# New duration estimates, and new ranks and lookaheads, for the list scheduler of a two-layer hybrid encoder

## The chip, the cores and the metric

The kernel runs as one program on one core of a Trainium2 chip. The metric is the device time of one execution in microseconds (us). Five instruction streams of the core matter here: TensorE (PE in the profile, with PEld for its weight loads), VectorE (DVE), ScalarE (ACT), GpSimd (POOL) and SyncE (SP), which issues the DMAs. Each takes its instructions in the order in which the program gives them; semaphores tie the streams together.

## The reference, cut to what matters

The input x is (1, 512, 1024) float32; there are two layers. Each layer is

```
proj = h @ w_in                      # 1024 -> A 512 | B 512 | C 512 | D 352
o_a  = silu(LN(conv31(a * sigmoid(a'))))            # group A, depthwise, width 31
o_b  = softmax(rope(rms(q)) rope(rms(k))^T / 8) v   # group B, 4 heads of 64, 2 kv heads
o_c  = u * (W_s LN(v) + b), gelu before             # group C, chunks of 128 positions
o_d  = softmax(q_d k_d^T) v_d                       # group D, 4 heads, low-rank q and kv
h    = LN(alpha * h + concat(o_a..o_d) @ w_out)
up   = conv3(h @ ffn_w_up)                          # 1024 -> 2 x 2816
h    = LN(alpha * h + (silu(up_1) * up_2) @ ffn_w_down)
```

All of it is float32. The kernel holds float32 accuracy by splitting both factors of a product in a high part (rounded to fp32r) and a low part (the rest), and by three matmuls for each product: high by high, low by high, high by low.

## The kernel before

**Tiles.** The 512 positions are four tiles of 128 (`h` 0 to 3 in the program; the lists of instructions call their buffers h_83 to h_86). Weights come from HBM in chunks of two 512-column pieces, into three `raw` buffers. For each piece ACT writes the high part (`wh<-raw`), and DVE the low part (`wl<-raw,wh`); for the chunks of U, V and O (two low-rank matrices of group D, and the output projection) POOL writes the low part. Activations are transposed by PE into PSUM (`wk<-ident,h`) and split there by ACT and DVE into `hh` and `hl`. PSUM holds four `acc` and four `wk` buffers.

**Work of a layer.** Sections, in the order of the program: the projections `b`, `a`, `d`; `b_rope` (square roots `ny` on DVE, scalings `by` on ACT, products `bz` on DVE and `bw` on POOL), `b_heads`; `d_norm`, `d_lat`, `d_up` (group D's low-rank products; its rotary key products `kr` are small POOL operations); `b_att`; `c` (projection and gelu), `c_norm` (`svh`, `svl`), `c_sgu`; `d_att`; `conv` (62 DVE operations `aconv` in two chains, on the two halves of group A), `a_norm`, which begins with PE's transposes of `aconv`; then `out` (output projection and layer norm), `ffn` and `down`. In an attention, two heads go as a pair: for each, scores into `acc`, a maximum (`max<-acc`, DVE), exponentials with their sums (`prob<-acc,max`, ACT), transposes, split (`pth` on ACT, `ptl` on DVE), product with v, `bo` or `do`; at the end of a pair the sums' reciprocals `rec` and `mixh`, `mixl`. The spatial weights of `c_sgu` are split once in a layer: `sguh` on ACT, `sgul` on DVE.

**What sets the order.** Nothing is issued while the program is written: `Sched.record` notes 3830 operations with what they read and write. `Sched.place` then puts them in one order, as a list scheduler: it keeps a clock for each engine, takes for every operation the duration that `Sched.cost` gives it, and picks on each engine, among the operations that could begin first, the one with the lowest priority number. That number is the operation's place in the program plus the `rank` of its section; for weight splits it is the place at which a chunk `lead` chunks earlier is first used. `ahead` says how many chunks before its use a chunk's DMA may be issued, `window` how far from the oldest open operation an operation may be. `Sched.issue` issues the result (line 610, where all instructions of the trace stand). On the chip each engine keeps that order, and waits where its operands are not there yet; the numbers of `cost` have no other effect.

Of the kernel before, what the change touches and what calls it, by code (L numbers as in the profile page):

```python
# [48 lines left out]
for _k in KEYS:  # L49
# [22 lines left out]
TUNE = {'window': 334,  # L72
         'slack': 0.0,
         'spare': 1,
         'ahead': {'A': 6,
                   'B': 10,
                   'D': 10,
                   'U': 21,
                   'V': 12,
                   'C': 44,  # L80
                   'O': 5,
                   'F': 2,
                   'W': 6,
                   'W1': 35,
                   'W0': 15,
                   'C0': 42,
                   'A1': 17,
                   'V0': 17,
                   'C1': 42,
                   'F1': 6,  # L90
                   'A0': 30,
                   'B1': 34,
                   'D0': 9,
                   'F0': 5,
                   'B0': 27,
                   'V1': 28,
                   'U1': 32,
                   'U0': 40,
                   'D1': 5},
         'lead': {'A': 32,  # L100
                  'B': 14,
                  'D': 45,
                  'U': 73,
                  'V': 8,
                  'C': 0,
                  'O': 5,
                  'F': 37,
                  'W': 8,
                  'D1': 5,
                  'A0': 11,  # L110
                  'U1': 69,
                  'C1': 11,
                  'O1': 0,
                  'D0': 22,
                  'B1': 15,
                  'F1': 16,
                  'O0': 2,
                  'U0': 84,
                  'V1': 15,
                  'V0': 15,  # L120
                  'C0': 13,
                  'B0': 3,
                  'F0': 45,
                  'A1': 30,
                  'W0': 14,
                  'W1': 6},
         'rank': {'.0': 23,
                  '.1': -404,
                  '.3': -339,
                  'a0': 33,  # L130
                  'a1': 72,
                  'a_norm0': -14,
                  'b0': -1,
                  'b0.0': -212,
                  'b0.1': 256,
                  'b0.2': 81,
                  'b0.3': -477,
                  'b1': -618,
                  'b1.2': -365,
                  'b1.3': 59,  # L140
                  'b_att0': 142,
                  'b_att0.00': -455,
                  'b_att0.01': 19,
                  'b_att0.0n': 962,
                  'b_att0.10': -33,
                  'b_att0.1n': 49,
                  'b_att1': 24,
                  'b_att1.00': -25,
                  'b_att1.01': -10,
                  'b_att1.1n': 8,  # L150
                  'b_heads0': -527,
                  'b_heads0.0': 159,
                  'b_heads0.1': -3,
                  'b_heads1': 182,
                  'b_heads1.0': -174,
                  'b_heads1.1': -110,
                  'b_heads1.2': -4,
                  'b_rope0': -265,
                  'b_rope1': 794,
                  'c0': 78,  # L160
                  'c0.0': -15,
                  'c0.1': 6,
                  'c0.3': -638,
                  'c1': -66,
                  'c1.0': -131,
                  'c1.1': -9,
                  'c1.3': 150,
                  'c_norm0': 237,
                  'c_norm1': -16,
                  'c_sgu0': -22,  # L170
# [152 lines left out]
class Sched:  # L323
# [121 lines left out]
    def cost(eng, method, args, kw, outs, ins):  # L445
# [5 lines left out]
        n = max([v.arr.size for v in views])  # L451
# [1079 lines left out]
```

## Time and profile before

| | |
|---|---|
| time, median of 3 runs | 1155.11 us (1154.3 to 1155.8) |
| the profiled execution | 1155.01 us, of which the profile's span is 1153.2 us |
| busy: PE, DVE, ACT, POOL | 1131.9, 771.0, 558.2, 169.4 us |
| PE instructions | 5802 matmuls and transposes |

The span is what the profile sees; some 1.8 us of the execution lie around it. An engine's busy time says how much work it has, not what it is worth: the two layers alternate between stretches with different limits, so each is read by itself.

### The profile page before, as it was taken

What the parts mean: (1) busy time and instruction counts of PE and PEld (TensorE: products, weight loads), DVE (VectorE), ACT (ScalarE), POOL (GpSimd) and SP (SyncE); (2) the same over time, 40 slices, a digit from 0 to 9 for tenths busy, and PEclk for the clock granted to TensorE, in tenths of its full rate; (3) what the DMA queues carried; (4) which work ended last, traced back from release to release, by engine and by line L of the source; (5) the groups of instructions that cost most, each with busy time, mean ns of one, the idle gap of its engine ahead of it and who ended that gap; (6) DMA issues with size and microseconds to landing.
All of it is one profiled execution on the core that took longest, in us unless ns stands there. A gap on an engine that the chain in (4) does not pass through costs nothing.

```text
span 1153.2 us, 15412 instructions
## 1 busy us (share of the span) xinstructions
PE 1131.9 (98%) x5802; PEld 959.7 (83%) x5802; DVE 771.0 (67%) x1307; ACT 558.2 (48%) x1203; POOL 169.4 (15%) x203
## 2 busy tenths in 40 slices
PE   6999999999999999999999999999999999999997
PEld 5888888988888888888889877889888888888886
DVE  7799996776666755245667999777776656551425
ACT  5759794254444543224254679733564444431221
POOL 5324324100000001000112734320000000000002
PEclk9999999999999999999999999999999999999999
DMA  6520022233233532135232002122353223231311
GB/s 228 165 74 20 19 92 74 74 97 104 92 92 109 167 106 79 55 110 166 95 124 68 7 20 58 53 92 73 128 164 111 92 92 110 74 110 42 105 56 73
DMA packets 32041, 105.71 MB, mean 92 GB/s; under 512 B 3680, under 2 KB 4064, under 8 KB 31968
## 3 DMA queue, kind: packets, MB, share of 16 engines
q1 hardware_dynamic: 31968, 104.74, 27.7%
q8 instruction: 45, 0.74, 0.3%
q14 instruction: 28, 0.23, 0.1%
HBM read 102.63 MB, written 2.10 MB: 91 GB/s over the span
## 4 chain that ended last, share of the span: by engine, by line
PE 90%; ACT 5%; DVE 2%; DMA 1%; issue 1%; POOL 0%; SPq 0%; DVEq 0%; ACTq 0%
PE acc L610 55%; PE wk L610 35%; ACT prob L610 2%; ACT pth L610 1%; ACT wh L610 1%; DVE ptl L610 1%; ACT c L610 1%; DVE aconv L610 0%; DMA raw<-in_wst_dram 0%; DMA h<-in_x_dram 0%; ACT do L610 0%; DVE max L610 0%; DVE bo L610 0%; ACT mixh L610 0%; ACT bo L610 0%
## 5 line engine op out<-in xcount | busy, mean ns | idle before, releaser
L610 DVE TENSOR_TENSOR wl<-raw,wh 128x512 fp32r<-128x512 f32 (+1 forms) x264 | 171.6, 688 | 85.6 <-ACT wh L610 60.6
L610 ACT ACTIVATE wh<-raw 128x512 fp32r<-128x512 f32 (+2 forms) x310 | 176.1, 615 | 67.8 <-DMA raw<-in_wst_dram 60.8
L610 PE MATMUL acc<-hh,wh 128*128 128x512 f32 (+1 forms) x544 | 191.8, 353 | 0.0
L610 PE MATMUL acc<-hh,wl 128*128 128x512 f32 (+1 forms) x544 | 191.2, 352 | 0.0
L610 PE MATMUL acc<-hl,wh 128*128 128x512 f32 (+1 forms) x544 | 191.2, 352 | 0.0
L610 PE MATMUL wk<-hh,wh 128*128 128x512 f32 x320 | 124.5, 389 | 0.0
L610 PE MATMUL wk<-hl,wh 128*128 128x512 f32 x320 | 124.5, 389 | 0.0
L610 PE MATMUL wk<-hh,wl 128*128 128x512 f32 x320 | 124.5, 389 | 0.0
L610 PEld LDWEIGHTS acc<-hh,wl 128*128 128x128 f32 x544 | 102.8, 189 | 13.8
L610 PEld LDWEIGHTS acc<-hl,wh 128*128 128x128 f32 x544 | 102.9, 189 | 13.6
L610 PEld LDWEIGHTS acc<-hh,wh 128*128 128x128 f32 x544 | 102.9, 189 | 13.6
L610 POOL TENSOR_TENSOR vr<-ve,mhalf 128x1 f32<-128x1 f32 (+2 forms) x26 | 25.4, 977 | 534.6 <-DVE ve L610 534.5
L610 DVE SCALAR_TENSOR_TENSOR y<-acc,pp,y 128x511 f32<-128x511 f32 x96 | 71.6, 749 | 37.2 <-ACT y L610 35.4
L610 DVE TENSOR_TENSOR hl<-raw,hh 128x512 fp32r<-128x512 f32 x56 | 37.7, 689 | 84.3 <-ACT hh L610 84.2
L610 ACT ACTIVATE hh<-raw 128x512 fp32r<-128x512 f32 x56 | 34.9, 630 | 111.5 <-PE acc L610 93.5
L610 DVE SCALAR_TENSOR_TENSOR aconv<-aglu,pp,aconv 128x501 f32<-128x501 f32 (+14 forms) x120 | 86.7, 758 | 0.6
L610 PE MATMUL acc<-hl,fh 128*128 128x512 f32 x224 | 85.8, 383 | 0.0
L610 PE MATMUL acc<-hh,fh 128*128 128x512 f32 x224 | 85.7, 383 | 0.0
L610 PE MATMUL acc<-hh,fl 128*128 128x512 f32 x224 | 85.7, 382 | 0.0
L610 DVE SCALAR_TENSOR_TENSOR y<-wk,pp,y 128x511 f32<-128x511 f32 x80 | 60.0, 750 | 33.7 <-ACT y L610 31.9
L610 PE MATMUL wk<-wh,hh 128*128 128x512 f32 (+1 forms) x192 | 73.7, 384 | 0.0
L610 POOL TENSOR_TENSOR wl<-raw,wh 128x512 fp32r<-128x512 f32 (+1 forms) x46 | 59.8, 1320 | 91.6 <-ACT wh L610 58.3
(201 smaller groups left out, 2290.5 us busy)
## 6 DMA issues: line engine op xcount, KB each, us to landing
raw<-in_wst_dram SPq DMA_DIRECT2D x172, 512.0 KB, 3.5
row<-in_rows_dram SPq DMA_DIRECT2D x16, 256.0 KB, 5.0
raw<-in_wst_dram SPq DMA_DIRECT2D x8, 352.0 KB, 3.0
out_dram<-h SPq DMA_DIRECT2D x8, 256.0 KB, 2.0
h<-in_x_dram SPq DMA_DIRECT2D x3, 512.0 KB, 5.2
raw<-in_wst_dram SPq DMA_DIRECT2D x2, 384.0 KB, 3.8
h<-in_x_dram SPq DMA_DIRECT2D x2, 256.0 KB, 3.1
raw<-in_wst_dram SPq DMA_DIRECT2D x2, 256.0 KB, 3.1
```

The source lines that it names most:

```text
L610: f(*[a.real() if isinstance(a, View) else a for a in args], **{k: v.real() if isinstance(v, View) else v for k, v in kw.items()})
```

## The change

It edits two things: the estimates in `cost`, and the tables in `TUNE` that `place` uses. An exponential over 512 columns with its sum now counts 30 ns above its plain cost in place of 115. A POOL product counted 150 ns plus 1.66 or 2.1 ns for an element; it now counts 150 ns up to 8 elements, and 320 ns plus 1.4 or 1.8 ns for an element above. `window`, 20 of the 25 `ahead` numbers, all `lead` numbers and nearly all `rank` entries are new.

```diff
-TUNE = {'window': 334,
+TUNE = {'window': 591,
...
-                   'C0': 42,
+                   'C0': 62,
...
-            return ((50.0 if from_psum else 94.0) + n / 1.2 + 72.0 * ptrs + (115.0 if "accum_out" in kw else 0.0),
+            return ((50.0 if from_psum else 94.0) + n / 1.2 + 72.0 * ptrs + ((30.0 if n == 512 else 115.0) if "accum_out" in kw else 0.0),
                     118.0 if from_psum else 95.0, False)
         if ALU.pow in args:
             return 700.0 + n * 145.0, 40.0, True
         narrow = any(0 in v.arr.strides for v in ins)
-        return 150.0 + n * (1.66 if narrow and n == 512 else 2.1), 40.0, True
+        if n <= 8:
+            return 150.0, 40.0, True
+        return 320.0 + n * (1.4 if narrow and n == 512 else 1.8), 40.0, True
```

The same 3830 operations are issued, with the same dependences; only their order on each engine, and the buffers that they get, differ. Of DVE's 1307 places 905 hold another operation than before, of ACT's 1064 places 787, of POOL's 196 places 69, of SP's 222 places 132. PE's order differs in six stretches of the program: the start, the attention part of both layers, the beginning of the feed-forward part of both, and the boundary of the layers. From the middle of layer 1's feed-forward part on PE's order is the same to the end. At the start SP now issues the spatial weights of layer 0 and their rows (`sguraw`, `sgurow`, 256 KB each) ahead of the first chunk of A, and DVE splits `sgul` there, 84 places earlier; tile h_85 is normalised before h_86, which was the other way round. Three places show the rest; the numbers in a name are those of a buffer.

On DVE in layer 0's `b_rope`, where the roots `ny` end and the rope products `bz` begin, stood (`raw_527` is the first chunk of C)

```order
L610 TENSOR_TENSOR nu_577<-nu_577,hv_539 128x24
L610 SCALAR_TENSOR_TENSOR ny_584<-nu_577,ny_566 128x24
L610 TENSOR_SCALAR ny_584<-ny_584 128x4x4
L610 TENSOR_TENSOR wl_596<-raw_527,wh_581 128x512
L610 TENSOR_TENSOR wl_599<-raw_527,wh_594 128x512
L610 TENSOR_TENSOR bz_613<-by_275,btab_246 128x256
```

and there stands now (`raw_530` is the first chunk of C, `raw_539` the second)

```order
L614 TENSOR_TENSOR nu_582<-nu_582,hv_549 128x24
L614 TENSOR_TENSOR wl_594<-raw_530,wh_576 128x512
L614 SCALAR_TENSOR_TENSOR ny_596<-nu_582,ny_580 128x24
L614 TENSOR_TENSOR wl_605<-raw_530,wh_591 128x512
L614 TENSOR_SCALAR ny_596<-ny_596 128x4x4
L614 TENSOR_TENSOR wl_614<-raw_539,wh_607 128x512
L614 TENSOR_TENSOR wl_623<-raw_539,wh_610 128x512
L614 TENSOR_TENSOR bz_629<-by_289,btab_259 128x256
```

so the last two steps of the roots, for which ACT's scalings wait, now stand behind splits of C's first chunk, and the second chunk's splits ahead of the rope products.

On DVE in layer 0's `d_att`, up to the last maximum of the last pair of heads (`acc_2017`, `do_1846` is the output of the pair before), stood

```order
L610 TENSOR_REDUCE max_1995<-acc_1960 128x1
L610 TENSOR_REDUCE max_2045<-acc_2016 128x1
L610 TENSOR_TENSOR do_1846<-wk_1950,do_1846 64x256
L610 TENSOR_TENSOR do_1846<-wk_1999,do_1846 64x256
L610 TENSOR_TENSOR do_2055<-wk_2035,do_2055 64x256
L610 TENSOR_TENSOR c_1543<-c_1543,sgurow_1013 128x256
L610 TENSOR_REDUCE max_2045<-acc_2017 128x1
L610 TENSOR_TENSOR ptl_2079<-wk_2049,pth_2070 128x512
```

and there stands now (`do_1847` is the output of the pair before)

```order
L614 TENSOR_TENSOR do_1847<-do_1847,wk_1956 128x512
L614 TENSOR_REDUCE max_2002<-acc_1967 128x1
L614 TENSOR_REDUCE max_2055<-acc_2016 128x1
L614 TENSOR_TENSOR mixl_2066<-do_1847,mixh_2048 128x512
L614 TENSOR_TENSOR do_2057<-wk_2034,do_2057 64x256
L614 TENSOR_TENSOR ptl_2081<-wk_2050,pth_2068 128x512
L614 TENSOR_TENSOR ptl_2085<-wk_2059,pth_2079 128x512
L614 TENSOR_REDUCE max_2055<-acc_2017 128x1
```

so the end of the pair before (`rec`, `do`, `mixl`) and two `ptl` moved ahead of the last maximum, and four `svl` and two `c` of `c_norm` behind it.

On PE at the boundary of the layers, where layer 1's first projection takes tile h_85 in, stood

```order
L610 MATMUL wk_5470<-wh_5258,hl 128x512
L610 MATMUL wk_5499<-wh_5232,hh 128x512
L610 MATMUL wk_5499<-wl_5238,hh 128x512
L610 MATMUL wk_5499<-wh_5232,hl 128x512
L610 MATMUL wk_5499<-wh_5236,hh 128x512
L610 MATMUL wk_5499<-wl_5246,hh 128x512
L610 MATMUL wk_5499<-wh_5236,hl 128x512
L610 MATMUL wk_5511<-ident,h_85 128x128 x4
L610 MATMUL wk_5519<-ident,h_85 128x128 x4
```

and there stands now

```order
L614 MATMUL wk_5472<-wh_5192,hh 128x512
L614 MATMUL wk_5472<-wl_5202,hh 128x512
L614 MATMUL wk_5472<-wh_5192,hl 128x512
L614 MATMUL wk_5498<-ident,h_85 128x128 x4
L614 MATMUL wk_5510<-ident,h_85 128x128 x4
L614 MATMUL wk_5472<-wh_5226,hh 128x512
```

so the six matmuls of the next tile's group that stood ahead of the transposes of h_85 now come behind them.

## Rows read from the trace of the kernel before

**Rows 1.** The page: span and busy times.

```profile
span 1153.2 us, 15412 instructions
PE 1131.9 (98%) x5802; PEld 959.7 (83%) x5802; DVE 771.0 (67%) x1307; ACT 558.2 (48%) x1203; POOL 169.4 (15%) x203
```

**Rows 2.** Busy time by stage; columns PE, PEld, DVE, ACT, POOL, clock, DMA.

```profile
60.00:174.00 114.00, 111.54 (x691) 95.61 (x690) 110.91 (x205) 89.02 (x224) 37.31 (x51) 1.00 0.16 52
174.00:570.00 396.00, 396.00 (x1865) 332.40 (x1864) 234.06 (x364) 158.66 (x262) 19.52 (x19) 1.00 0.32 103
...
632.00:739.00 107.00, 103.92 (x653) 89.29 (x652) 103.22 (x191) 84.92 (x215) 45.77 (x48) 1.00 0.13 40
739.00:1080.00 341.00, 341.00 (x1623) 286.87 (x1622) 201.19 (x311) 141.70 (x236) 15.98 (x15) 1.00 0.30 96
```

**Rows 3.** The same, of three stretches inside the two attention stages.

```profile
128.00:152.00 24.00, 21.82 (x140) 18.36 (x139) 22.76 (x42) 23.28 (x51) 13.06 (x11) 1.00 0.37 118
...
632.00:660.00 28.00, 28.00 (x166) 25.25 (x165) 27.75 (x45) 14.80 (x48) 18.59 (x13) 1.00 0.06 20
...
690.00:731.00 41.00, 38.51 (x243) 32.52 (x242) 38.65 (x75) 39.33 (x89) 12.44 (x10) 1.00 0.25 77
```

**Rows 4.** Waits of PE in 134 to 152 us.

```profile
PE wk L610 <- DVE bo L610: 1.1, 1, 1.1
PE acc L610 <- ACT prob L610: 0.9, 2, 0.5
```

**Rows 5.** Start-up by windows, as Rows 2.

```profile
18.00:19.00 1.00, 1.00 (x5) 0.80 (x4) 1.00 (x3) 0.00 (x0) 0.44 (x1) 0.50 1.04 410
...
25.00:30.00 5.00, 5.00 (x32) 4.25 (x31) 4.89 (x9) 4.30 (x20) 0.00 (x0) 1.00 0.02 5
```

**Rows 6.** Timeline of DVE in layer 0's rope: start, us, instruction.

```profile
46.62 0.18 DVE L610 TENSOR_SCALAR ny<-ny 128x16 f32<-128x16 f32 x1
48.02 1.29 DVE L610 TENSOR_TENSOR wl<-raw,wh 128x512 fp32r<-128x512 f32 x2 [1.23 <-ACT wh L610]
...
60.47 0.54 DVE L610 TENSOR_SCALAR aconv<-aglu,pp 128x512 f32<-128x512 f32 x1
```

**Rows 7.** Timeline of ACT, the same place.

```profile
48.41 5.84 ACT L610 ACTIVATE by<-by,ny 128x64 f32<-128x64 f32 x24
```

**Rows 8.** End of the convolution: DVE and PE, layers 0 and 1.

```profile
171.20 1.51 DVE L610 SCALAR_TENSOR_TENSOR aconv<-aglu,pp,aconv 128x498 f32<-128x498 f32 x2
...
173.35 1.03 PE L610 MATMUL wk<-ident,aconv 128*128 128x128 f32 x8
...
736.48 1.51 DVE L610 SCALAR_TENSOR_TENSOR aconv<-aglu,pp,aconv 128x498 f32<-128x498 f32 x2
...
738.71 1.18 PE L610 MATMUL wk<-ident,aconv 128*128 128x128 f32 x8
```

**Rows 9.** Tiles ptl and svl: instructions with least, median and longest ns.

```profile
L610 DVE TENSOR_TENSOR ptl<-wk,pth x64: 637/681/693, 82.4 to 735.5; 128x512 fp32r<-128x512 f32 x64
...
L610 DVE TENSOR_TENSOR svl<-c,svh x16: 273/284/294, 156.1 to 736.3; 128x128 fp32r<-128x128 f32 x16
```

**Rows 10.** Timeline of PE, DVE, POOL at the layers' boundary.

```profile
582.59 0.39 PE L610 MATMUL wk<-wh,hh 128*128 128x512 f32 x1
...
583.95 1.07 PE L610 MATMUL wk<-ident,h 128*128 128x128 f32 x8
...
577.12 3.22 DVE L610 TENSOR_TENSOR wl<-raw,wh 128x512 fp32r<-128x512 f32 x2
...
582.85 1.40 DVE L610 SCALAR_TENSOR_TENSOR h<-h,vr,row 128x512 f32<-128x512 f32 x2
...
585.56 1.29 DVE L610 TENSOR_TENSOR wl<-raw,wh 128x512 fp32r<-128x512 f32 x2
...
576.91 2.88 POOL L610 TENSOR_TENSOR wl<-raw,wh 128x384 fp32r<-128x384 f32 x2
```

**Rows 11.** The tile kr, columns as Rows 9.

```profile
L610 POOL TENSOR_TENSOR kr<-dc,tabs x24: 215/658/12032, 61.3 to 655.4; 128x16 f32<-128x16 f32 x16, 128x32 f32<-128x32 f32 x8
```

More of the change, by code (lines that the diff above doesn't have):

```diff
@@ L67 @@
 POOL_FIRST = [(i, j) for i in range(4) for j in range(2)]
-TUNE = {'window': 334,
+TUNE = {'window': 591,
          'slack': 0.0,
          'spare': 1,
[L75 to L78, printed above, removed]
+         'ahead': {'A': 17,
+                   'B': 21,
+                   'D': 1,
+                   'U': 24,
                    'V': 12,
-                   'C': 44,
+                   'C': 20,
                    'O': 5,
[L82 to L85, printed above, removed]
-                   'C0': 42,
-                   'A1': 17,
-                   'V0': 17,
-                   'C1': 42,
+                   'F': 8,
+                   'W': 10,
+                   'W1': 22,
+                   'W0': 10,
+                   'C0': 62,
+                   'A1': 9,
+                   'V0': 15,
+                   'C1': 20,
@@ L90 @@
                    'F1': 6,
-                   'A0': 30,
+                   'A0': 45,
                    'B1': 34,
[L93 to L98, printed above, removed]
-                   'D1': 5},
[L100 to L126, printed above, removed]
@@ new lines @@
+                   'D0': 10,
+                   'F0': 6,
+                   'B0': 29,
+                   'V1': 17,
+                   'U1': 41,
+                   'U0': 26,
+                   'D1': 5},
+         'lead': {'A': 29,
+                  'B': 12,
+                  'D': 26,
+                  'U': 82,
+                  'V': 2,
+                  'C': 7,
+                  'O': 16,
+                  'F': 40,
+                  'W': 23,
+                  'D1': 2,
+                  'A0': 0,
+                  'U1': 45,
+                  'C1': 30,
+                  'O1': 1,
+                  'D0': 12,
+                  'B1': 13,
+                  'F1': 26,
+                  'O0': 0,
+                  'U0': 89,
+                  'V1': 6,
+                  'V0': 18,
+                  'C0': 6,
+                  'B0': 29,
+                  'F0': 49,
+                  'A1': 44,
+                  'W0': 46,
+                  'W1': 0},
```

184 lines of the change are left out of this document (93 added, 91 removed).

## The prediction

> **What bounds the kernel now.** I read the page first: PE is busy 1131.9 of 1153.2 us [rows 1], so no order of the same instructions can take off more than the 21 us in which it isn't. Then the busy times by stage, to see where those 21 us lie. In the feed-forward and down stages PE is busy 396.00 of 396.00 and 341.00 of 341.00 us [rows 2]: a new order has nothing to gain there, it can only lose. In the two attention stages, 60 to 174 and 632 to 739 us, PE misses 114 - 111.54 = 2.5 and 107 - 103.92 = 3.1 us, and DVE is busy 110.91 and 103.22 us of them, 97 and 96% [rows 2]; the rest of the 21 lies at the start, where data has to arrive, and in the last layer norm. Cut finer, PE's loss lies in two stretches only: 128 to 152 us (2.2 us lost) and 690 to 731 us (2.5 us lost), and there ACT is busy too, 23.28 of 24 and 39.33 of 41 us [rows 3]. The reader is to see that three engines are full at once: while the last heads are worked off, a head's chain goes PE, DVE (maximum), ACT (exponential), PE, ACT, DVE, PE, and none of the three has room to serve it at once. The waits name it: PE waits there for `bo` on DVE 1.1 us and for `prob` on ACT 0.9 us [rows 4].
>
> How a stage ends decides what a gain inside it is worth. The convolution's last instructions on DVE end at 171.20 + 1.51 = 172.71 us, and PE takes their transposes at 173.35; in layer 1 these are 737.99 and 738.71 [rows 8]. So DVE and PE come to the end of a stage within 0.64 and 0.72 us of each other. Whatever frees only one of them gains at most that.
>
> The sum is made against the profiled execution, 1155.01 us, of which 1153.2 is the span; the median of the runs, 1155.11, is 0.1 above it.
>
> **The new estimates themselves** cost nothing on the chip, they only steer, and they are not simply nearer to it: the rotary products `kr` took from 215 to 12032 ns, 658 in the middle [rows 11], and the estimate for one of 32 elements goes from 217 to 378 ns. So I judge the order that comes out, place by place.
>
> **Start-up: 0 us (-0.1 to +0.8).** The two new 256 KB loads ahead of A's first chunk delay that chunk, and a split of it now stands on DVE ahead of the end of h_85's normalisation; h_85's transposes now come first on PE. PE is busy in all of 18 to 19 and of 25 to 30 us; in the first the granted clock reads 0.50 [rows 5], the lower of its two levels, 1.2 GHz. What looks like slow matmuls there is the clock and not a wait that could be taken out. Reordering work on an engine that never waits gives nothing; should the late chunk hold DVE up, the loss is bounded by the one split ahead of it with its hand-off, some 0.8 us.
>
> **Layer 0's rope: DVE 0.45 us later, 0 us on the end (0 to +0.5).** Before, the roots are ready at 46.62 + 0.18 = 46.8 us, and ACT's 24 scalings run from 48.41 for 5.84 us [rows 6, 7]. In the new order the last two root steps wait behind the splits of C's first chunk, which DVE could begin only at 48.02, after 1.23 us idle for ACT's part [rows 6]; the second chunk's splits go ahead too. Two such splits take 1.29 us and two root steps 0.36, so the roots end near 48.02 + 1.29 + 0.36 = 49.7 and the scalings begin some 1.5 us later. The second chunk's splits, 1.29 us, are then done already, which leaves 0.2; ACT's scalings now pace all four rope products, for which I add 0.4: the convolution starts near 61.1 instead of 60.47 [rows 6], 0.6 later. Of the work ahead of it `sgul` (one split, 0.65 us) is done in addition, and one rope product of 384 columns (three quarters of a split, 0.5 us) is not: 0.6 - 0.65 + 0.5 = 0.45 us behind. The 62 convolution operations and everything else that stands ahead of their last one are the same set in both orders (one `do` apart in layer 1), so this goes through to the end of the convolution: 172.71 + 0.45 = 173.16, still before 173.35 [rows 8]. The cover is those 0.64 us; if they are gone, it costs 0.45.
>
> **Last heads of both layers: 0 us (-2.3 to +1.7).** Ahead of layer 0's last maximum DVE now has seven instructions more and seven fewer. Two `ptl`, a `do` and a `mixl` come, 512 columns each, 4 x 0.68 us [rows 9], with `rec`, as small as the root steps (0.18) [rows 6], and one `aconv` net (1.51 / 2) [rows 8]; four `svl` go, 4 x 0.28 [rows 9], and two `c` of 256 columns, some 0.4 each, between the two. 2.72 + 0.18 + 0.75 - 1.12 - 0.8 = 1.7 us of work more. In layer 1, four of 512 columns (two `mixl`, a `bo`, a `do`) and two `do` of 256 go from there, and three `svl` and a `c` come: 2.72 + 0.8 - 0.84 - 0.4 = 2.3 us less. What comes earlier in one place is missing later, since DVE's set up to the end of the convolution is the same; a gain or loss shows at the end only as far as DVE's idle time, 3.1 and 3.8 us in the two stages [rows 2], changes. With opposite signs and no more evidence I take nothing, and keep both ends.
>
> **Boundary of the layers: +0.1 us (-0.3 to +0.5).** PE's transposes of h_85 start at 583.95, behind six matmuls that start at 582.59 [rows 10] and now come after them, so they could start at 582.6. DVE writes h_85's two halves from 582.85 on, 1.40 us for both [rows 10]. DVE's order ahead of them changes little: the two splits at 577.12 are now three, but only one POOL split runs beside them. Those two took 3.22 us where two take 1.29 elsewhere, while POOL ran two for 2.88 [rows 10]; with one disturbed (1.5 us) and two not, DVE gets to the halves some 0.4 us earlier, the first being ready near 583.05. PE then waits about 0.6 us in a place where it did not. Against it, `sgul` of layer 1 (0.68 us) leaves DVE's full stretch and is done in this slack one. PE comes to the end of the stage 0.6 us later at most, DVE 0.68 us earlier; as they end within 0.72 us of each other [rows 8], I book +0.1.
>
> Sum: 0 + 0 + 0 + 0.1 on 1155.01 gives **1155.1 us**: no change that can be measured. A measurement of this kernel tells about 0.2%, 2.3 us, from nothing.
>
> **A rule that speaks against the change.** The rows show DVE and POOL slowing each other: the 3.22 us beside 2.88 [rows 10], and one `kr` product of 12.03 us [rows 11] in a stretch where DVE is busy 27.75 of 28 us [rows 3]. The Trainium skill, SBUF — State Buffer, in the section SBUF: two separate sides, says that the pair of ports which DVE and GpSimd share is an exclusive lock: an instruction of the one with two SBUF inputs holds it to its end, and the other waits. The trace agrees with that direction; no duration per element, old or new, can describe it. By it the sum is that of the first rival, 1156.1; by the rows alone it stays 1155.1.
>
> **Rivals.** *The lock moves with the order (within the forecast's class).* At the boundary the one POOL split meets the two halves of h_85 on DVE instead of the splits. The excess of 3.22 - 1.29 = 1.9 us for two POOL splits gives about 1.0 for one, on the path that PE now waits on: 1156.1. For it: the halves now start earlier and POOL's split of that time is still to come. Against it: POOL's split was over at 576.91 + 2.88 = 579.8, 3 us before.
>
> *Faster: the last heads find DVE free.* In layer 1 the last maximum has 2.3 us less of DVE's work ahead of it, so its exponential can start earlier; the 2.5 us that PE loses in 690 to 731 [rows 3] would mostly go, and with them DVE's idle time. If half of the idle time of both stages goes, (3.1 + 3.8) / 2 = 3.5 us: 1151.6. Against it: that work is not gone, it stands behind the maximum now and is due by the same end of the convolution.
>
> *Slower: layer 0's last exponential comes late.* The 1.7 us of DVE's work ahead of the last maximum come before its exponential, and ahead of that ACT has more work too: three instructions of 512 columns come (`pth`, `mixh`, `recs`) and two short `svh` go, priced like DVE's of those sizes 3 x 0.65 - 2 x 0.28 = 1.4 us, in the layer where ACT is busy 97% as the last heads begin [rows 3]. If the two delays add up, the last head's product, the output projection that needs it and the layer norm come 3.1 us later: 1158.2. It decides when PE has less than those 3.1 us of other matmuls to lay in; the output projection's first chunks are such work, which speaks against it. For it: PE found nothing to lay in for 2.2 us in 128 to 152 [rows 3].
>
> That the change does nothing is no case of its own: the order differs in most places, and with equal ends it gives the forecast's time.
>
> **Chances and range.** Forecast with the lock's case: 0.46 (the lock alone 0.08). Faster case: 0.30, since either stage may give it and DVE's idle is there to be had. Slower case: 0.24. The range takes in the bounds of the terms and most of both outer cases: below, 1155.1 - 0.1 - 2.3 - 0.4 and half of layer 0's idle time, 1.5, is 1150.8; above, 1155.1 + 0.8 + 0.5 + 1.7 + 0.4 = 1158.5. The forecast's own range is 1153.4 to 1156.8.
>
> **What would show it.** Right: in the new profile PE has no waits in 18 to 30 us; the last `aconv` of layer 0 ends near 173.1 and its transposes begin at about 173.4; the scalings of the rope begin near 49.9; PE waits some 0.6 us for `h` at 582.6; the span is within 1 us of 1153.2. Wrong: a convolution that ends more than 1 us earlier or later in either layer, or DVE idle in a stage that differs by more than 1 us from 3.1 and 3.8; then the place of the last heads decides, by what PE waits for in 128 to 152 and 690 to 731. A loss in 174 to 570 or 739 to 1080, where PE never waited, would be something that none of these cases holds.

## The result, and the profile of the changed kernel

| | before | changed |
|---|---|---|
| time, median | 1155.35 us | 1162.01 us (1161.5 to 1163.3, 4 runs) |
| ratio | | 1.0058, 95% interval 1.0042 to 1.0074 |
| the profiled execution | 1155.01 us, span 1153.2 | 1163.34 us, span 1161.6 |

The changed kernel is 6.7 us slower; the forecast was no change, with a range that ended at 1158.5. The profiled execution is the slowest of the four.

The page, in answer to [rows 1]:

```profile
span 1161.6 us, 15408 instructions
...
PE 1136.3 (98%) x5802; PEld 961.6 (83%) x5802; DVE 771.7 (66%) x1307; ACT 556.3 (48%) x1203; POOL 154.1 (13%) x203
```

DVE's work is the same (771.0 before, 771.7 now), and POOL's busy time has fallen, by 15.3 us. PE executes as many matmuls as before and is busy 4.4 us longer, so only half of the 8.4 us between the two spans shows as idle time of PE. Busy time by stage, in answer to [rows 2]; columns PE, PEld, DVE, ACT, POOL, clock, DMA. The bounds are shifted by what the kernel is late by then, 3 to 6 us in layer 0 and 8 in layer 1, but the attention windows don't hold exactly the instructions of before; their busy times show the kind of loss, and the table below gives its size:

```profile
63.00:180.00 117.00, 113.40 (x693) 95.52 (x692) 110.31 (x203) 87.82 (x223) 33.80 (x50) 1.00 0.14 46
180.00:576.00 396.00, 395.87 (x1862) 332.23 (x1860) 235.65 (x363) 158.25 (x262) 19.74 (x20) 1.00 0.33 104
640.00:747.00 107.00, 102.08 (x642) 87.67 (x641) 101.25 (x188) 85.37 (x218) 34.94 (x48) 1.00 0.15 50
747.00:1088.00 341.00, 341.00 (x1625) 287.03 (x1624) 200.84 (x311) 139.77 (x231) 15.95 (x15) 1.00 0.30 96
```

The feed-forward stages are as full as before, to 0.13 us. In the attention stages PE now misses 3.6 and 4.9 us (2.5 and 3.1 before), and DVE 6.7 and 5.8 (3.1 and 3.8). That both engines miss more says only that the stages got longer with the same work in them; it doesn't say which of the two is late for the other.

The size is read from three marks on PE: the first matmul of A's projection, and the transposes that begin `a_norm` in either layer. They split the kernel into a start, a stretch with layer 0's attention, and one with layer 1's (layer 0's feed-forward in it). Before, they stand at 39.66, 173.35 and 738.71 us; now:

```profile
42.64 0.39 PE L614 MATMUL acc<-hh,wh 128*128 128x512 f32 x1
...
179.19 1.03 PE L614 MATMUL wk<-ident,aconv 128*128 128x128 f32 x8
...
747.16 1.04 PE L614 MATMUL wk<-ident,aconv 128*128 128x128 f32 x8
```

So 2.98 us were lost by the first mark, 136.55 - 133.69 = 2.86 in layer 0, and 567.97 - 565.36 = 2.61 in layer 1: 8.45 of the 8.4 us between the two spans. The busy times of the three stretches, before and then now (columns as above):

```profile
0.00:39.66 39.66, 30.99 (x145) 25.39 (x145) 29.63 (x58) 22.33 (x73) 15.99 (x24) 0.96 0.63 216
39.66:173.35 133.69, 131.23 (x782) 112.49 (x780) 125.17 (x239) 105.93 (x282) 49.08 (x69) 1.00 0.20 65
173.35:738.71 565.36, 562.28 (x2904) 477.65 (x2903) 381.84 (x643) 275.04 (x593) 79.78 (x89) 1.00 0.27 89
```

```profile
0.00:42.64 42.64, 33.11 (x144) 27.19 (x145) 30.07 (x59) 23.51 (x78) 16.56 (x24) 0.92 0.66 220
42.64:179.19 136.55, 132.95 (x781) 112.27 (x780) 124.68 (x237) 103.70 (x277) 43.30 (x68) 1.00 0.18 57
179.19:747.16 567.97, 562.88 (x2903) 477.88 (x2902) 383.44 (x643) 276.50 (x600) 69.64 (x90) 1.00 0.28 89
```

In the start, 2.1 of the 2.98 us are PE busy longer, at a granted clock of 0.92 in place of 0.96, and 0.9 are idle time. In layer 0, PE is busy 1.7 us longer at the full clock and idle 1.1 us longer, while DVE does as much as before and stands 3.4 us longer (8.52 and 11.87 us). In layer 1 PE is busy 0.6 and idle 2.0 us longer. Part of the longer busy time is waiting that the profile shows as work: the bar of a matmul of 512 columns is 0.39 us long where the next one starts 0.23 us later, so a short wait lies under the bar (an example stands with the boundary of the layers below). That this is all of layer 0's 1.7 us isn't shown.

The start scatters from execution to execution (below). The other two stretches scatter less: with the order of a layer left as it was, layer 0 has 133.37 to 133.69 us before and 136.55 to 136.66 in the changed order, layer 1 has 565.22 to 565.36 and 567.76 to 568.85. PE's waits at the last heads of layer 1, 698 to 747 us:

```profile
PE wk L614 <- DVE ptl L614: 1.4, 4, 0.7
PE wk L614 <- DVE bo L614: 1.1, 1, 1.1
PE acc L614 <- ACT prob L614: 0.8, 1, 0.8
PE wk L614 <- DVE do L614: 0.6, 1, 0.6
PE wk L614 <- ACT pth L614: 0.5, 1, 0.5
```

They are the links of a head (its steps from engine to engine), as in [rows 4], one after the other. In layer 0 a loss stands where there was none: PE was busy in all of 90 to 135 us before, and loses a microsecond now in the stretch with group D's low-rank products and the second pair of heads of B. Before and, 3 us later, now:

```profile
90.00:105.00 15.00, 15.00 (x90) 12.59 (x90) 14.78 (x29) 13.94 (x41) 7.71 (x15) 1.00 0.01 2
105.00:120.00 15.00, 15.00 (x94) 12.83 (x93) 14.84 (x29) 12.63 (x26) 5.01 (x8) 1.00 0.11 36
120.00:135.00 15.00, 15.00 (x85) 12.75 (x85) 14.52 (x26) 8.64 (x17) 5.30 (x4) 1.00 0.07 16
```

```profile
93.00:108.00 15.00, 15.00 (x99) 12.35 (x96) 14.18 (x22) 11.84 (x28) 3.66 (x6) 1.00 0.38 123
108.00:123.00 15.00, 13.97 (x90) 10.64 (x90) 13.40 (x31) 14.36 (x40) 8.36 (x17) 1.00 0.11 37
123.00:138.00 15.00, 14.89 (x79) 12.24 (x79) 14.91 (x27) 9.21 (x18) 2.08 (x2) 1.00 0.00 0
```

### The profile page after: what moved, and what is told of

Its sections match the earlier page's. It is cut to its first block, busy times and chain, and to the rows that moved or that the text cites. A ratio compares the mean times of both kernels' runs of the same rounds, so it can differ in the third digit from the quotient of the medians.

```text
span 1161.6 us, 15408 instructions
## 1 busy us (share of the span) xinstructions
PE 1136.3 (98%) x5802; PEld 961.6 (83%) x5802; DVE 771.7 (66%) x1307; ACT 556.3 (48%) x1203; POOL 154.1 (13%) x203
## 4 chain that ended last, share of the span: by engine, by line
PE 86%; ACT 7%; DVE 4%; DMA 1%; issue 1%; POOL 0%; SPq 0%; DVEq 0%; ACTq 0%
PE acc L614 54%; PE wk L614 32%; ACT prob L614 2%; ACT pth L614 1%; ACT wh L614 1%; DVE ptl L614 1%; DVE aconv L614 1%; ACT c L614 1%; DVE h L614 1%; DMA h<-in_x_dram 1%; DVE max L614 0%; DMA raw<-in_wst_dram 0%; ACT L614 0%; ACT bo L614 0%; ACT do L614 0%
## 5 line engine op out<-in xcount | busy, mean ns | idle before, releaser
L614 DVE SCALAR_TENSOR_TENSOR aconv<-aglu,pp,aconv 128x507 f32<-128x507 f32 (+14 forms) x120 | 85.7, 755 | 0.7
L614 PE MATMUL wk<-wh,hl 128*128 128x512 f32 (+1 forms) x192 | 72.0, 375 | 0.1
```

Of the source, the lines that this page charges most:

```text
L614: f(*[a.real() if isinstance(a, View) else a for a in args], **{k: v.real() if isinstance(v, View) else v for k, v in kw.items()})
```

## The experiments

All of them issue the same operations; only the order differs, so nothing is left out in any of them. Two helpers were added to the scheduler. `graft(first, rest, n)` takes the first n operations of one order and the others in the sequence of a second. `move` gives some operations the place of another one in a finished order and keeps the rest; an operation that finds no free buffer there comes as soon as there is one. `slots` then deals out the buffers again. `OLD` is the old table, and `placed(OLD, False)` the old order, made with the old estimates. Numbers are those of operations as they are recorded.

The table gives the medians, and from each run's profile the three marks: the time of the first, and the lengths of the two stretches up to the second and third.

| run | median, us | ratio to before, 95% interval | start | layer 0 | layer 1 |
|---|---|---|---|---|---|
| before | 1155.4 | | 39.66 | 133.69 | 565.36 |
| changed | 1162.0 | 1.0042 to 1.0074 | 42.64 | 136.55 | 567.97 |
| g_l0 | 1159.9 | 1.0029 to 1.0054 | 42.03 | 136.66 | 565.90 |
| g_l1 | 1157.6 | 1.0011 to 1.0031 | 41.32 | 133.37 | 568.42 |
| g_start | 1167.7 | 1.0092 to 1.0119 | 40.54 | 143.30 | 568.02 |
| cost_only | 1173.7 | 1.0142 to 1.0170 | 42.16 | 146.84 | 568.00 |
| cover0 | 1165.7 | 1.0078 to 1.0105 | 42.17 | 140.87 | 567.76 |
| cover1 | 1165.7 | 1.0075 to 1.0102 | 41.78 | 136.59 | 571.07 |
| evac | 1162.7 | 1.0054 to 1.0079 | 42.58 | 136.58 | 568.04 |
| three | 1170.0 | 1.0109 to 1.0140 | 42.35 | 140.84 | 571.50 |
| c_early | 1165.0 | 1.0068 to 1.0096 | 39.89 | 143.50 | 565.34 |
| conv_early | 1158.8 | 1.0019 to 1.0040 | 40.80 | 136.82 | 565.29 |
| c_conv | 1166.4 | 1.0084 to 1.0115 | 40.31 | 144.45 | 565.22 |
| pair_late | 1157.8 | 1.0016 to 1.0034 | 42.24 | 133.41 | 567.58 |
| sgu_first | 1158.7 | 1.0020 to 1.0043 | 43.69 | 134.20 | 565.23 |
| bfill | 1156.1 | 1.0001 to 1.0020 | 39.72 | 135.65 | 564.47 |
| fill | 1162.0 | 1.0046 to 1.0071 | 42.12 | 136.92 | 568.17 |
| wh_late | 1162.6 | 1.0047 to 1.0072 | 40.47 | 137.26 | 568.08 |
| sgu_back | 1162.0 | 1.0040 to 1.0068 | 40.61 | 136.57 | 568.85 |
| both_back | 1173.9 | 1.0144 to 1.0171 | 40.35 | 149.73 | 567.79 |

**Where it is lost: one part of the order at a time.**

```diff
-        self.order = s.place(TUNE)
+        self.order = s.slots(*s.graft(s.placed(OLD, False), s.placed(TUNE), 168))      # g_start
+        self.order = s.slots(*s.graft(s.placed(OLD, False), s.placed(TUNE), 1283))     # g_l1
+        self.order = s.slots(*s.graft(s.placed(TUNE), s.placed(OLD, False), 1269))     # g_l0
```

The cut of the last two lies in layer 0's feed-forward, at 300 us; that of the first at 36 us.

> The changed order for its first 1269 operations (start and layer 0's attention), then the order of before: what the change does to the start and layer 0 alone. Theory 1: 1155.35 and about 4.7, so 1160 (1159 to 1161). Rival (the parts don't add, since a late layer 0 is made up for later): 1157 to 1158.

> The order of before for its first 1283 operations (layer 0 with its start and attention, to about 300 us), then the changed order: what the change does to layer 1 alone. Theory 1: 1155.35 and about 2, so 1157.3 (1156.5 to 1158.2). Rival, layer 1 gains by the 2.3 us of DVE work moved behind its last maximum, as the faster case had it: 1153 to 1155.

> The order of before for its first 168 operations (to about 36 us), then everything else in the changed order, with the changed buffers. Theory 1, the loss comes in three places (start-up about 2 us by the drift of PE's start times, layer 0's attention about 3, layer 1's about 2): the start-up's part goes, 1160 us (1159 to 1161). Rival, the loss sits in the attention stages alone and the late start in the profile is chance of that one execution: no change against the changed kernel, 1162.

g_l0 costs 4.4 us and g_l1 2.1, 6.5 together of the 6.7: the losses add up, and each layer has its own. g_start says nothing of the start: its seam cost 6.8 us in layer 0 (143.30 against 136.55), with a wait of PE for `bz` of 3.6 us and a granted clock of 0.50 behind it. The start is better read from the first mark of all profiles. With the old order of the start, eight profiles have it at 39.66 to 42.24 us, 40.6 on average; with the new one, seven (changed, g_l0, cover0, cover1, fill, wh_late, both_back) at 40.35 to 42.64, 41.7 on average. So the start costs about 1.1 us, less than one execution scatters, and 1.1 + 2.86 + 2.61 = 6.6 agrees with the medians. It isn't the clock alone: among the profiles whose start reads the same 0.96, four with the old order have the mark at 40.3 on average and five with the new one at 41.7.

**The estimates alone.** The new `cost` with the old table:

```diff
-        self.order = s.place(TUNE)
+        self.order = s.slots(*s.placed(OLD))
```

> The old ranks, lookaheads, leads and window with the new duration estimates: the first of the two edits alone. If ranks are fitted to the estimates they were searched with, any other estimates give a worse order: 1157 to 1161. Rival, the new estimates are simply better and the new ranks are what loses: 1155 or less.

It costs 18 us, 13 of them in layer 0. So the old table is worth its time only with the old estimates. The other half of the change, the new table with the old estimates, wasn't run, so how the 6.7 us divide between estimates and tables isn't shown.

**One part taken out of the changed order.** From the traces I had three suspects: PE's independent matmuls (C's second group, 571 to 574) stand too early in layer 0; the end of the second pair of heads (2430 to 2433) and the output projection's product that needs it (2793) too late in layer 1; and at the start ACT's evacuations `by` between weight splits.

```diff
+        order, end = s.placed(TUNE)
+        for what, before in [([571], 490), ([572], 500), ([573], 503), ([574], 464)]:      # cover0
+        for what, before in [([2430], 2596), ([2431], 2605), ([2432], 2607), ([2433], 2612), ([2793], 2681)]:  # cover1
+        for what, before in [([102, 108, 103, 104, 105, 106, 109], 160)]:                  # evac
+            order, end = s.move(order, end, [s.ops[i] for i in what], s.ops[before])
+        self.order = s.slots(order, end)
```

> The changed order with one thing back near its old place, in layer 0: the four matmul groups of C's second tile, which the change brought ahead of group D's up-projections, stand again between the attention products that follow those. Theory 2 (attention with nothing else between its links fills DVE, ACT and PE by turns, and PE waits on each link): the stretch from the up-projections to the first `d_att` goes from 3.4 us of waiting back to about 1.3, so 1160.0 us (1159.3 to 1160.7) against 1162.0. Rival (DVE's work up to the end of the convolution sets the end, wherever the matmuls stand): no change, 1162.

> The changed order with one thing back near its old place, in layer 1: the end of `b_att`'s second pair (transposes of `recs`, `bo`, `mixh`, `mixl`), and so the output projection's group that needs it, stand again before the last heads' products instead of behind them. Theory 2: PE has that group to lay in between the last head's links, and loses 1 to 1.7 us less, 1160.6 us (1160 to 1161.2) against 1162.0. Rival (the 1.6 us of DVE work that go ahead of the last maximum again cost as much as the cover gives): 1162 or more.

> The changed order with ACT's order at the start edited: the evacuations `by` of the first projection's first tile stand together, ahead of five of the splits `wh` of A's first chunks. Theory 2 for the start: PE's transposes of h_86 wait 1.2 us for the last of these evacuations, which frees their PSUM buffer; without it about 0.8 to 1.2 us go, 1161 us (1160.6 to 1161.4). Rival (the late landings of the start's loads set PE's start): 1162.

> The three edits together. If the three places are independent, as the first runs' layer 0 and layer 1 added up: the sum of the three gains, 1162.0 - 2.0 - 1.4 - 1.0 = 1157.6 us (1156.8 to 1158.8). Rival (they share a wait): no better than the best of them alone.

None of the expected gains came; the rivals of cover1, evac and three held. cover0 and cover1 cost another 3.6 and 3.7 us, evac changes nothing, and all three together cost 8.0, the sum. In the changed kernel PE waits at 30.79 us for a PSUM buffer that ACT's last `by` has to free:

```profile
28.58 1.04 PE L614 MATMUL wk<-ident,h 128*128 128x128 f32 x8
30.79 1.09 PE L614 MATMUL wk<-ident,h 128*128 128x128 f32 x8 [1.17 <-ACT by L614]
```

In evac that wait is gone, and PE stands as long at the next set, for a split on DVE:

```profile
27.80 2.10 PE L834 MATMUL wk<-ident,h 128*128 128x128 f32 x12 [0.32 <-issue]
30.93 0.33 PE L834 MATMUL wk<-ident,h 128*128 128x128 f32 x1 [1.03 <-DVE hl L834]
```

Two more took out waits of DVE and of ACT. fill puts the next operation of the convolution ahead of five instructions on DVE that wait for ACT or POOL; wh_late puts two weight splits on ACT from between the heads' links to where ACT has room.

```diff
+        for what, before in [([843], 321), ([861], 411), ([862], 505), ([2749], 2286), ([2724], 2427)]:  # fill
+        for what, before in [([899, 901], 590)]:                                           # wh_late
```

> The changed order, DVE alone edited: at five places where DVE waits for ACT or POOL (0.61, 0.55 and 0.62 us in layer 0, 0.33 and 0.70 in layer 1; 2.8 us together) the next operation of the convolution, whose operands are there, is put ahead of the waiting instruction. Theory that DVE's time is what the stage is short of: the idle time goes and most of it comes off the end, about 1159.5. Theory that the ring of a head's links (PE, DVE, ACT, PE) is what is short, and PE's cover: an instruction of 0.65 us ahead of a link of which PE waits makes that link as late as the wait did, so 1162 with no gain, or a little more.

> The changed order, ACT alone edited: two weight splits for the output projection, which stand on ACT at 115.4 us of layer 0 between the links of two heads, where ACT is busy 14.68 of 15 us, are put some 8 us later, where ACT has room (9.23 of 15 us); before, they stood at 104.9 us, and PE needs their chunk at 165 us. Theory that ACT's links are late in the bare stretch: the wait of 0.62 us for the split of the probabilities at 118.27 and PE's of 0.93 behind it shrink, 1161.2. Theory of PE's cover alone, with the other links as late: 1162.0.

Neither gives anything. That fill's operations made the links behind them as late as the waits did is what its expectation said and fits the result; it isn't read from the trace.

**One part put into the order of before.**

```diff
+        order, end = s.placed(OLD, False)
+        for what, before in [([571, 572], 441), ([573], 345), ([574], 359)]:               # c_early
+        for what, before in [([850, 851, 852], 443), ([853, 854], 350), ([855, 856, 857], 372)]:  # conv_early
+        for what, before in [([2430], 2693), ([2431], 2690), ([2432], 2689), ([2433], 2690), ([2793], 2759)]:  # pair_late
+        for what, before in [([586, 587], 157), ([588], 101), ([589], 140)]:               # sgu_first
+        for what, before in [([2703], 2004), ([2704], 2087), ([2724], 2286), ([2755], 2417), ([869], 539)]:  # bfill
```

c_conv has the moves of c_early and conv_early.

> The order of before, with one part of the change alone, on PE: in layer 0 the four products of C's second group are brought forward, from 110 to 117 us to where the new order has them, among the products of the heads and ahead of group D's low-rank products; no other engine's order is touched. Theory of the cover (PE waits in the attention stretches because the independent matmuls that used to lie between a head's products have been used up earlier): PE gets as bare in 104 to 117 us as in the new order and the loss there is some 2 us, 1157.3. Rival (the order of PE doesn't matter as long as DVE and ACT have the same work in the same order, since they set the pace there): 1155.3, no change.

> The order of before, with another part of the change alone, on DVE: eight operations of layer 0's convolution (some 0.65 us each), which lie between 91 and 114 us, are brought forward by 1 to 15 us, to before 99 us, as the new order has them; no other engine's order is touched. Theory that DVE's fillers are what counts (the convolution is work that DVE can do while the heads' next link is with ACT; done early, it makes the early links late and leaves DVE idle later): DVE's idle time in 100 to 120 us, 0 before, becomes some 2 us, 1157.3. Rival, the cover on PE alone: DVE does the same work by 115 us, so 1155.3 to 1155.8.

> The order of before with both of the parts that were tried alone: C's second group early on PE (+9.5 us alone, DVE idle for 5.3 us at 98 to 104 since group D's products came late) and eight operations of the convolution early on DVE (+3.3 alone). Theory that the two belong together (while PE does the matmuls brought forward, DVE does the convolution brought forward, and neither waits for the other): clearly less than the sum, +3 to +6, 1158.5 to 1161.5, and DVE's idle time at 98 to 104 mostly filled. Rival (each costs by itself what it takes from the heads' links): the sum, +12.8, 1168.

c_early touches PE alone and costs 9.5 us; its four products found no buffer earlier and came in one block, ahead of group D's low-rank products, which is coarser than the changed order. Its busy times, columns as above:

```profile
98.00:104.00 6.00, 6.00 (x30) 5.07 (x29) 0.65 (x2) 2.32 (x7) 1.74 (x5) 1.00 0.00 0
104.00:130.00 26.00, 25.25 (x149) 20.01 (x148) 24.65 (x48) 19.93 (x46) 10.44 (x18) 1.00 0.06 21
...
132.00:137.00 5.00, 0.90 (x6) 0.42 (x4) 5.00 (x8) 1.72 (x4) 2.94 (x2) 0.98 0.13 14
137.00:140.00 3.00, 2.13 (x8) 1.73 (x9) 3.00 (x6) 1.76 (x4) 0.05 (x1) 0.50 0.39 152
140.00:142.00 2.00, 2.00 (x6) 1.61 (x6) 0.78 (x2) 0.91 (x2) 2.00 (x2) 0.50 0.00 0
```

This is the mechanism in its plainest form. In 98 to 104 us PE is busy throughout and DVE stands: nothing looks lost on PE. DVE's wait there, and PE's 30 us later:

```profile
103.82 0.49 DVE L834 TENSOR_TENSOR dv<-wk,dv 128x128 fp32r<-128x128 f32 x2 [5.35 <-PE wk L834]
...
137.09 1.11 PE L834 MATMUL wk<-ident,prob 128*128 128x128 f32 x4 [4.19 <-DVE dl L834]
```

DVE has no room to make up 5.35 us (busy 14.8, 14.8 and 14.5 of 15 us in 90 to 135 before), so PE gets the bill when its own supply has run out. DVE's order is that of before, so the same instruction can be compared: counted from the first mark, this `dv` begins 5.0 us later than before (103.82 - 39.89 against 98.59 - 39.66), and the `dl` that PE waits for 8.7 us later (136.36 and 127.48). Some 1.8 of the further 3.7 us aren't waits: three convolution operations ahead of that `dl` take 1.68 and 2.27 us, where they took 0.72 and 1.40, beside two splits on POOL.

```profile
132.44 1.68 DVE L834 SCALAR_TENSOR_TENSOR aconv<-aglu,pp,aconv 128x503 f32<-128x503 f32 x1
134.16 2.27 DVE L834 SCALAR_TENSOR_TENSOR aconv<-aglu,pp,aconv 128x502 f32<-128x502 f32 x2
132.31 2.94 POOL L834 TENSOR_TENSOR wl<-raw,wh 128x512 fp32r<-128x512 f32 x2 [17.21 <-ACT wh L834]
```

conv_early touches DVE alone, does the same work on DVE by 115 us, and still costs 3.3 us: the links behind the convolution's operations are late, and in 93 to 108 us PE stands for two microseconds.

```profile
93.00:108.00 15.00, 12.99 (x68) 9.48 (x66) 13.53 (x28) 11.75 (x34) 6.50 (x12) 1.00 0.01 2
```

That is as much as the changed order loses in all of layer 0 (136.82 and 136.55). c_conv costs 11.2: nearly the sum. The idea that the one part covers the other fell.

> The order of before with layer 1's part alone: the end of the last pair of heads of group B (one transpose on PE, bo, mixh, mixl) and the product of the output projection that needs it go behind the last heads of group D, where the new order has them. Theory that they were the work which covers the last heads' links: PE waits some 1.5 us more in 700 to 738 us, 1157. Rival, from the opposite move in the changed order, which cost 3.7 us (the 1.6 us of DVE's work ahead of the last maxima are what hurts): the last maxima come earlier, and 1154 to 1155.

pair_late costs 2.5 us, all in layer 1 (567.58; g_l1 568.42). Measured from its first mark, DVE's convolution ends 740.15 - 42.24 = 697.9, no later than before (737.99 - 39.66 = 698.3), and yet `a_norm` begins 743.23 - 42.24 = 701.0, later than 699.05: PE's own chain, with the moved product behind the last head, ends last.

> The order of before with the start's part alone: the spatial weights of layer 0 and their rows are loaded ahead of A's first chunk, and split on ACT and DVE in the start, as the new order has them. Theory that the start's loss comes from the PSUM buffers and the order of ACT's evacuations, which stay as they were here: 1155.5 (the same), and with two splits less in DVE's and ACT's full stretches rather 1155. Rival (the loads and splits delay A's first chunk): +1.5, 1157.

The rival won, and by more: +3.4 us. ACT and PE at its start (ACT first; the next fence is PE):

```profile
19.92 0.60 ACT L834 ACTIVATE hh<-wk 128x512 fp32r<-128x512 f32 x1 [1.23 <-PE wk L834]
23.71 0.63 ACT L834 ACTIVATE wh<-raw 128x512 fp32r<-128x512 f32 x1 [3.20 <-DMA raw<-in_wst_dram]
24.25 0.61 ACT L834 ACTIVATE sguh<-sguraw 128x512 fp32r<-128x512 f32 x1
24.77 0.20 ACT L834 ACTIVATE by<-wk 128x64 f32<-128x64 f32 x1
```

```profile
27.88 1.36 PE L834 MATMUL wk<-ident,h 128*128 128x128 f32 x6 [2.52 <-issue]
```

The first chunk of A lands later behind the two loads; ACT, which takes its instructions in order, stands 3.2 us at its split with the evacuations `by` queued behind; and PE, whose four `wk` buffers they have to free by the program, stands 2.52 us (the profile names no releaser there).

> The changed order with the start's part taken out: the spatial weights of layer 0 and their rows are loaded behind A's four chunks and split on ACT and DVE when the first chunks of D are; all else as changed. Theory, from the opposite move in the order of before, which cost 3.4 us (PE idle 2.5 us at 25 to 28 since ACT stood waiting for A's first chunk with the evacuations of B's first tile behind it): the start's loss of 1.3 to 1.8 us goes, 1160.4. Rival (the changed order has the evacuations ahead of that split, so the loads cost it nothing, and its loss lies in the order of the tiles): 1162.0.

The rival won again: taking the same part out of the changed order gives nothing, since there `by` stands ahead of that split. Its PE still waits 1.2 us for `by`.

> The order of before, DVE alone edited as in fill: at five places where DVE waits for ACT or POOL (0.37 us in layer 0, 0.61, 0.88, 0.55 and 0.51 in layer 1; 2.9 us together) the next operation of the convolution is put ahead of the waiting instruction. From fill, which gave nothing: 1155.5, no change. If DVE's time is short in this order after all: 1153 to 1154, faster than both kernels.

No gain in all: 0.9 us less in layer 1, 2.0 more in layer 0, where one operation of 0.65 us was put ahead of the last `bo` of a pair. PE waits 2.2 us for that `bo`, where it waited 1.1, and the granted clock then reads 0.50 in 139.8 to 143.1 us, so part of the 2.0 is the clock. Its four moves in layer 1 alone weren't tried; in this one profile filled gaps did give time there, so not every such gap is bound to its link.

```diff
+        moves = [([571], 490), ([572], 500), ([573], 503), ([574], 464)] + [([i], b) for i, b in neighbours]   # both_back
```

where `neighbours` puts 24 operations of layer 0's convolution (827 to 833 and 850 to 866; the expectation says 23) each ahead of the instruction that it preceded in the old order.

> The changed order with both of layer 0's parts taken out: C's second group back between the heads' products on PE (alone +3.6 us on the changed order) and 23 operations of the convolution back to the neighbours that they had before on DVE. Theory that the two belong together: DVE's fillers are then there when PE does C's group, and it comes out at least no slower than the changed order, 1159 to 1162. Rival, from the sum that both gave in the order of before (each moved alone or with the other only costs, because the rest of the order is fitted to where they stand): slower, 1164 to 1168.

It is 12 us slower than the changed kernel, more than the rival said; in the profile all of it lies in layer 0, where PE waits 5.3 us for one `ptl` and the granted clock reads 0.50 behind that.

## Why the prediction was wrong

**What bounds the kernel** was read rightly: the loss lies in the start and the two attention stages, and the feed-forward stages neither gained nor lost (395.87 and 341.00 us busy). The failing step is the way I summed inside a stage: "The 62 convolution operations and everything else that stands ahead of their last one are the same set in both orders, so this goes through to the end of the convolution", and "a gain or loss shows at the end only as far as DVE's idle time changes", for which I then took no change. Both of the prediction's own signs of being wrong came: the convolution of layer 0 ends 3.0 us later by the first mark, and DVE is idle 6.7 and 5.8 us in the two stages in place of 3.1 and 3.8. An equal set ends at an equal time only if DVE waits no longer on the way, and whether it waits is decided by the place of every link on PE and ACT. c_early left DVE's sequence as it was and cost 9.5 us; conv_early changed only DVE's sequence, with the same work done by 115 us, and cost 3.3; pair_late ended the convolution no later and the stage 2 us later. The end of the convolution still fits, in the changed kernel, within half a microsecond of PE (178.72 and 179.19), as [rows 8] said. That fits two engines driven by the same ring of links, and doesn't show that DVE's sum is what to count: in pair_late the two lie 3.1 us apart (740.15 and 743.23).

**Start-up, 0 us.** Wrong, by about 1.1. "Reordering work on an engine that never waits gives nothing" overlooked that PE can be made to wait: I bounded a late chunk by one split with its hand-off, 0.8 us, and did not ask what is queued behind that split on ACT. In the order of before it is the evacuation of PSUM, and costs 3.4 us (sgu_first). In the changed order it isn't, and there the wait is that for `by` and, once that is gone, for the next link (evac). Which of the start's moves carries the 1.1 us isn't shown.

**Layer 0's rope.** The convolution starts at 62.81 us, 2.3 after [rows 6], on a PE that is 3.0 late by its first mark: it is early by 0.6, not late by 0.6. ACT's scalings begin at 51.87, by the first mark 0.5 us later than before and not 1.5. What this place alone gives on the end isn't shown.

**Last heads, 0 us (-2.3 to +1.7).** The faster rival counted on layer 1, where the last maximum has 2.3 us less of DVE's work ahead. That work is the end of the pair before; late, it costs what pair_late shows, 2.5 us, a loss beyond this term's +1.7. Back in front of the last maxima (cover1) it costs 3.7 in the changed order. So the move is one sufficient way to lose what layer 1 lost, and taking it back alone is no cure. The slower rival had the right sign in layer 0 by the wrong place: the loss begins before the last heads, at 108 to 123 us.

**The boundary, +0.1**, was small as forecast. Matmuls of this kind start 0.23 us apart; from the last one ahead of the transposes of h_85 to these it is 0.40, so PE waits 0.2 us and not the 0.6 that I gave:

```profile
588.72 0.39 PE L614 MATMUL wk<-wh,hl 128*128 128x512 f32 x1
589.12 1.29 PE L614 MATMUL wk<-ident,h 128*128 128x128 f32 x8
```

**The lock's rival** can be set aside for the change: at the boundary DVE writes the two halves of h_85 in 1.41 us, as before (1.40, [rows 10]), DVE's busy time is the same in both kernels, and POOL's products got faster, as the tile `kr` shows beside [rows 11]. In c_early DVE's work beside POOL's splits did take 1.8 us longer.

```profile
588.23 1.41 DVE L614 SCALAR_TENSOR_TENSOR h<-h,vr,row 128x512 f32<-128x512 f32 x2
...
L614 POOL TENSOR_TENSOR kr<-dc,tabs x24: 215/235/824, 65.5 to 662.8; 128x16 f32<-128x16 f32 x16, 128x32 f32<-128x32 f32 x8
```

**What stays open.** Layer 0's 2.9 us are not put down to a move. Both suspects cost 3 us or more in the old order, so either is enough to lose that much, though c_early's block is coarser than the changed order and its 9.5 us hold the clock and the work that took longer beside POOL; neither gives it back when taken out of the new one, alone or together (cover0, both_back). That such orders are fitted as a whole would explain this; which of the changed places began the loss isn't shown.

## What to carry to other kernels

Where two or three engines are full at once and hand links to each other, don't compare sums of work up to a point: look for the engine that a move starves, even while the engine you care about is busy, because a full engine has no room to make the time up: in c_early the wait showed 30 us later on another one. For each transfer that is put ahead of another, follow the late one to its first reader and ask what stands behind that reader on its engine, down to the PSUM buffers that PE needs next. To test a suspect, put it into the good order as well as taking it out of the bad one: here none of the parts taken out of the new order gave time back, while all four put into the old one cost time, so a part that hurts where it is put need not help where it is taken away.

## What the runs showed of the hardware

A stop of PE in the middle of the kernel can cost more than its own length. In c_early the granted clock reads 1.00 up to PE's wait of 4.19 us at 132 to 137 us, and 0.50 in 137 to 142, that is 1.2 in place of 2.4 GHz. The same pair of matmuls took there

```profile
140.01 1.05 PE L834 MATMUL acc<-dh,dh 96*128 96x512 f32 x2
```

and 0.63 us at the full clock later in that trace, at 163.28. By the busy times, 4.1 us of PE's work in 137 to 142 at half the clock are 2 us lost on top of the wait. In sgu_first it falls too, after the wait of 2.52:

```profile
25.00:28.00 3.00, 0.47 (x3) 0.15 (x2) 1.95 (x6) 3.00 (x15) 0.55 (x1) 1.00 0.03 12
...
29.00:31.00 2.00, 2.00 (x8) 1.71 (x7) 2.00 (x5) 1.42 (x3) 0.00 (x0) 0.50 0.04 8
```

So a part of what c_early and sgu_first cost is the clock, and so it is in c_conv, g_start, cost_only and both_back, which read 0.50 behind waits of 3.5 to 5.3 us. In the profile of the changed kernel's attention stages, where the waits are at most 1.1 us each, it stays at 1.00. That isn't so in every execution of the same order: in sgu_back, whose layer 1 is the changed kernel's, it reads 0.50 behind the same wait for `bo`, there 1.2 us long,

```profile
705.00:708.00 3.00, 1.60 (x10) 1.00 (x9) 2.52 (x6) 2.90 (x9) 0.00 (x0) 1.00 0.00 0
708.60:712.00 3.40, 3.40 (x15) 3.00 (x14) 2.95 (x6) 2.67 (x7) 1.69 (x2) 0.50 0.00 0
```

and so it does in g_l1 and in three. Layer 1 took 568.85 us in sgu_back, against 567.76 to 568.08 in the six profiles of that order in which the clock stayed at 1.00: behind one and the same wait the clock falls in some executions and not in others, and where it fell it cost some 0.9 us.

The start scatters by 2.6 us between profiles of one order (39.66 to 42.24), and the clock is part of it: pair_late, the latest of the eight, reads, in 15 to 20 and 20 to 25 us,

```profile
15.00:20.00 5.00, 2.29 (x8) 2.00 (x9) 3.69 (x6) 1.75 (x3) 4.38 (x5) 0.67 1.00 293
20.00:25.00 5.00, 5.00 (x18) 4.04 (x17) 2.98 (x8) 1.82 (x6) 2.79 (x4) 0.65 0.58 235
```

and bfill, at 39.72, 1.00 in both. A difference of one or two microseconds in the start can't be read from one profile of each kernel.
